# Values of the last block: one expert of each token a row, added up on VectorE

## The chip, the cores and the metric

The kernel runs on one core of one Trainium2 chip. A core has five engines that run side by side, each with its own queue of instructions taken in order: TensorE (PE in the profile), VectorE (DVE), ScalarE (ACT), GpSimd (POOL) and SyncE (SP). SP and POOL mainly issue transfers, which 16 DMA engines carry out. The metric is the device time of one execution in microseconds (us); before the change it was 3333.57 us, the median of 3 runs (3333.47 to 3339.92).

## The reference, cut to what matters

The model is one block: a token mixer (two kinds of attention heads) over 16 meta tokens and 1024 tokens, a residual sum, and then a mixture of 16384 one-neuron experts with a width of 1024, float32 throughout. The change touches the expert part only:

```
# per block of 128 tokens; ids and gate: (128 tokens, 128 chosen experts)
u   = u_emb[ids]                                   # rows of 1024
act = gelu(einsum('ted,td->te', u, xb))            # one key product per token and expert
w   = gate * act
out = einsum('te,ted->td', w, v_emb[ids])          # weighted sum of 128 value rows per token
h_res = h_res + out
```

So each token takes 128 key rows and 128 value rows of 1024 numbers (4 KB), chosen by its own ids.

## The kernel before

The 1024 tokens are worked in four segments of 256 tokens (SEGS), each of two blocks of 128. The middle two segments (DENSE = (1, 2)) compute the experts densely: in a last loop over all 16384 experts, TensorE multiplies with the whole tables. The first and last segment gather: for each block, 128 transfers fetch the key rows and 128 the value rows (gather_rows, L313). The gathers of the last segment run under the dense loop, paced by it.

**The dense loop** (L1254 on) goes over 32 groups of 4 x 128 experts (GRP = 4). For a group, weights (L1215) multiplies the first layer's outputs with the gates (DVE w, L1224), splits each in two parts (ACT Wh, L1227; DVE Wl, L1228); dense_u (L1165) makes the first layer's tiles for a later group (AHEAD = 5 tiles ahead); dense_v (L1232) multiplies with the values in two halves of 512 columns (PE vo, L1246) and adds them up (DVE acc, L1251). A table tile comes through halves (L273): a transfer to raw by SP, a cast on ACT (wh, L279), a difference on DVE (wl, L284); there are four raw buffers (RAW) and two of wh and wl (WH). Of the 32 groups 12 have their first layer computed in earlier stages and stored (spill); for these dense_u only loads w and does a gelu, and TensorE has nothing to do in it. For the others it is 24 products a tile (PE du, L290). The order (L1160) takes 2 stored groups first, then computed ones until as many are left as stored ones, and then one of each in turn.

**The gathers under it.** gather_items (L395) fixes their order: the first block's 128 key rows; then by fours, the first block's values and the second block's keys; then the second block's 128 values. Paced (L1012) takes them: beat (L1198) is called after each first-layer tile (for two) and after each expert tile of dense_v (for one), and asks for 1.08 rows a beat (RATE), each request waiting for the last dense product issued so far; a row is used five steps after it was asked for (LAG). The rows lie in 11 buffers (GATH = 7 and GATHV = 4, room3 L1190).

- A key row tile holds the r-th expert of each token, one token a partition: POOL issues one indirect transfer with 128 row numbers (idx[:, lb, r]), and DVE multiplies it with the block's tokens and sums along the row into column r of actv (L335).
- A value row tile holds the 128 experts of one token, one expert a partition (ask_v, L349, L362). For this the ids are transposed once (idT). When four of them have come (use_v, L368), DVE copies four weight columns into an otherwise zero tile Z (L378), and TensorE multiplies Z with the rows into four groups of 32 columns, two halves each, adding up over 32 steps in G.po (L384); the profile counts 16 products a step. Ahead of the first step, weigh (L338) makes the weights: gelu on ACT, times gate, transposed on TensorE, copied to wT (L347). After the last, the residual comes from h2d into a row buffer, DVE adds G.po to it (L389), and SP stores it.

**What sets the order.** The program gives each instruction its place in the source order, and a planner with a simulated clock puts them in one fixed order for each engine before the kernel runs; dependences become waits. issue_after keeps a row's use behind the last dense product (for TensorE) and the last wl (for DVE) that were issued before it in the source.

Of the kernel before, what the change touches and what calls it, by code (L numbers as in the profile page):

```python
# [9 lines left out]
F32 = mybir.dt.float32  # L10
F32R = mybir.dt.float32r
I32 = mybir.dt.int32
U32 = mybir.dt.uint32
AF = mybir.ActivationFunctionType
OP = mybir.AluOpType
# [4 lines left out]
P = 128  # L20
D = 1024
KT = 8
# [5 lines left out]
NH_M = 4  # L28
# [8 lines left out]
def block_kernel(tc, I, out, dbg=None):  # L37
    nc = tc.nc
    with ExitStack() as ctx:
        _block_kernel(ctx, tc, nc, I, out, dbg)  # L40
# [6 lines left out]
NB = 2  # L47
# [33 lines left out]
GATH = 7  # L81
GATHV = 4

JV = 14

RATE = 1.08
# [5 lines left out]
def _block_kernel(ctx, tc, nc, I, out, dbg):  # L92

    def pool(name, bufs, stack=ctx, **kw):
        return stack.enter_context(tc.tile_pool(name=name, bufs=bufs, **kw))

    cp = pool("const", 1)
    big = pool("big", 1)
    wp = pool("wp", 2)
    pp = pool("peer", 2)  # L100
# [15 lines left out]
    st = pool("state", 1, front)  # L116
# [20 lines left out]
    dve, act, pe, pool_e, sync = nc.vector, nc.scalar, nc.tensor, nc.gpsimd, nc.sync  # L137
# [4 lines left out]
    identr = cp.tile([P, P], F32R, tag="identr", name="identr")  # L142
    dve.tensor_copy(identr, tmpi)
    ident = identr.bitcast(F32)
    negidr = cp.tile([P, P], F32R, tag="negidr", name="negidr")
    dve.tensor_scalar(negidr, tmpi, -1.0, None, op0=OP.mult)
    negid = negidr.bitcast(F32)
    tmpc = cp.tile([P, P], F32, tag="tmpc", name="tmpc")

    mask_st = cp.tile([P, P], F32R, tag="mask_st", name="mask_st")  # L150
    pool_e.memset(tmpc, 0.0)
    pool_e.affine_select(out=tmpc, in_=tmpc, compare_op=OP.is_ge, fill=-BIG, base=0,
                         pattern=[[1, P]], channel_multiplier=-1)
    dve.tensor_copy(mask_st, tmpc)

    tmpc2 = cp.tile([P, P], F32, tag="tmpc", name="tmpc2")
    mask_ts = cp.tile([P, P], F32R, tag="mask_ts", name="mask_ts")
    pool_e.memset(tmpc2, 0.0)
    pool_e.affine_select(out=tmpc2, in_=tmpc2, compare_op=OP.is_ge, fill=-BIG, base=0,
                         pattern=[[-1, P]], channel_multiplier=1)  # L160
    dve.tensor_copy(mask_ts, tmpc2)
    ones = cp.tile([P, P], F32, tag="ones", name="ones")
    pool_e.memset(ones, 1.0)
    blk2 = cp.tile([P, P], F32, tag="blk2", name="blk2")
    pool_e.memset(blk2, 0.0)
    pool_e.memset(blk2[0:64, 0:64], 1.0)
    pool_e.memset(blk2[64:128, 64:128], 1.0)
    eye4 = cp.tile([NH_M, NH_M], F32, tag="eye4", name="eye4")
    dve.tensor_copy(eye4, ident[0:NH_M, 0:NH_M])
    iota_i = cp.tile([P, P], I32, tag="tmpc", name="iota_i")  # L170
    pool_e.iota(iota_i, pattern=[[1, P]], base=0, channel_multiplier=0)
# [12 lines left out]
    for i in range(2):  # L184
        z = cp.tile([P, 4, 63], F32, tag=f"Z{i}", name=f"Z{i}")
# [3 lines left out]

    Zm = []  # L190
    for i in range(2):
        z = cp.tile([P, NB, 66], F32R, tag=f"Zm{i}", name=f"Zm{i}")
        zc = cp.tile([P, 66], F32, tag="tmpc", name="zc")
        pool_e.memset(zc, 0.0)
        pool_e.memset(zc[:, 64:65], -1.0)
        dve.tensor_copy(z, zc.unsqueeze(1).broadcast_to([P, NB, 66]))
        Zm.append(z)
    gmix = cp.tile([P, KT], F32, tag="gmix", name="gmix")
    sync.dma_start(gmix, I["g_mix"])
    gbias = cp.tile([72, 1], F32, tag="gbias", name="gbias")  # L200
    sync.dma_start(gbias, I["g_bias"])
    taps = cp.tile([P, 8, 4], F32, tag="taps", name="taps")
    sync.dma_start(taps, I["taps"])
    gqk = cp.tile([P, 2], F32, tag="gqk", name="gqk")
    sync.dma_start(gqk, I["g_qk"])
    gq8 = cp.tile([P, 1], F32, tag="gq8", name="gq8")
    dve.tensor_scalar(gq8, gqk[:, 0:1], 0.125, None, op0=OP.mult)
    epsc = cp.tile([P, 1], F32, tag="epsc", name="epsc")
    pool_e.memset(epsc, EPS)

    def rsqrt(o, x, scale, t):
# [28 lines left out]
    h2d = dp.tile([SEQ, D], F32, tag="h2d", name="h2d")  # L240
# [20 lines left out]
    for i in range(3):  # L261
        c = slice(i * 512, min(L, i * 512 + 512))
        for e, t in enumerate((oz, zo)):
            t = t[0:NH_F, 0:c.stop - c.start]
# [48 lines left out]
    def gather_rows(S, lb, share, room):  # L313

        b = S.xb0 + lb
        G = SimpleNamespace(S=S, lb=lb, b=b)
        G.actv = pp.tile([P, P], F32, tag="actv", name="actv")
        xn = []

        def ask(r):  # L320
            if r == 0:
                x_ = pp.tile([P, D], F32, tag="xng", name="xng", bufs=1)
                sync.dma_start(x_, xnd[b * P:(b + 1) * P, :])
                xn.append(x_)
            t = room("u", lb, r).tile([P, D], F32, tag="g", name="gu")
            d = pool_e.indirect_dma_start(out=t, out_offset=None, in_=I["peer_u"],  # L326
                                          in_offset=bass.IndirectOffsetOnAxis(ap=S.idx[:, lb, r:r + 1], axis=0))
            return t, d

        def use(r, t):  # L330
            if r % 16 in share:
                pool_e.tensor_tensor(t, t, xn[0], op=OP.mult)
                return lambda: act.activation(t, t, AF.Copy, accum_out=G.actv[:, r:r + 1])
            else:
                dve.scalar_tensor_tensor(t, t, 1.0, xn[0], op0=OP.mult, op1=OP.mult, accum_out=G.actv[:, r:r + 1])  # L335
        G.u = [(lambda r=r: ask(r), lambda t, r=r: use(r, t)) for r in range(P)]

        def weigh():  # L338
            wv = pp.tile([P, P], F32, tag="wv", name="wv", bufs=1)
            gelu = act.activation(wv, G.actv, AF.Gelu)  # L340
            with tc.issue_after(gelu.ins):
                act.preload_act_table_set(EXPLN)
            dve.tensor_mul(wv, wv, S.gate[:, lb, :])
            G.po = po_pool.tile([P, 2, 512], F32, tag="po", name="po")
            pe.transpose(G.po[:, 0, 0:P], wv, ident)
            G.wT = pp.tile([P, 4, 32], F32, tag="wT", name="wT", bufs=1)
            dve.tensor_copy(G.wT, G.po[:, 0, 0:P].rearrange("p (q j) -> p q j", q=4))  # L347

        def ask_v(tok):  # L349
            if S.idT is None:  # L350

                S.idT = []
                tp = po_pool.tile([P, 2, 512], F32, tag="po", name="idt")
                for k in range(NB):
                    idf = pp.tile([P, P], F32, tag="wv", name="idf", bufs=1)
                    dve.tensor_copy(idf, S.idx[:, k, :])
                    pe.transpose(tp[:, k, 0:P], idf, ident)
                    idT = pp.tile([P, P], I32, tag="idT", name="idT")
                    dve.tensor_copy(idT, tp[:, k, 0:P])
                    S.idT.append(idT)  # L360
            t = room("v", lb, tok % 32).tile([P, D], F32, tag="g", name="gv")
            d = pool_e.indirect_dma_start(out=t, out_offset=None, in_=I["peer_v"],  # L362
                                          in_offset=bass.IndirectOffsetOnAxis(ap=S.idT[lb][:, tok:tok + 1], axis=0))
            return t, d

        rows = {}

        def use_v(j, q, t):  # L368


            rows[q] = t
            if q < 3:
                return
            if j == 0:
                weigh()

            z = Zs[j % 2]
            dve.tensor_copy(z[:, :, 31:32], G.wT[:, :, j:j + 1])  # L378
            last = None
            with tc.high_priority():  # L380
                for n in range(2):
                    for q_ in reversed(range(4)):
                        with tc.issue_after(last.ins) if last else nullcontext():
                            last = pe.matmul(G.po[32 * q_:32 * q_ + 32, n, :], z[:, q_, 31 - j:63 - j],  # L384
                                             rows[q_][:, n * 512:(n + 1) * 512], start=(j == 0), stop=(j == 31))
            if j == 31:
                h2 = room("h", lb, j).tile([P, D], F32, tag="g", name="h2o")
                sync.dma_start(h2, h2d[b * P:(b + 1) * P, :])
                dve.tensor_add(h2, h2, G.po.rearrange("p a b -> p (a b)"))  # L389
                sync.dma_start(out[b * P:(b + 1) * P, :], h2)  # L390
        G.v = [(lambda tok=32 * q + j: ask_v(tok), lambda t, j=j, q=q: use_v(j, q, t))
               for j in range(32) for q in range(4)]
        return G

    def gather_items(S, share, room):  # L395

        A, B = (gather_rows(S, lb, share[lb], room) for lb in range(NB))
        yield from A.u
        for i in range(0, P, 4):
            yield from A.v[i:i + 4]  # L400
            yield from B.u[i:i + 4]
        yield from B.v
# [597 lines left out]
    def room0(kind, lb, i):  # L1000

        if kind == "v":
            return gpv if (i >= JV if lb == 0 else i % 2) else gp
        return gp
# [54 lines left out]
    for i in range(-1, len(SEGS)):  # L1059
# [9 lines left out]
        if i >= 0:  # L1069
            S = segs[i]  # L1070
# [114 lines left out]
    gbs.close()  # L1185
    mid.close()
    up = pool("ahead", AHEAD + 1, reuse_waits="tile")
    rows3 = [0]

    def room3(kind, lb, i):  # L1190
# [120 lines left out]
```

## Time and profile before

| what | value |
|---|---|
| median of the runs | 3333.57 us (3333.47 to 3339.92) |
| profiled execution, its own time | 3322.29 us |
| its span, first to last instruction | 3320.4 us |
| mean granted TensorE clock | 0.938 of full speed |
| busy: PE, DVE, ACT, POOL | 3004.0, 2210.0, 1060.2, 1375.3 us |
| moved by DMA | 931.18 MB, mean 280 GB/s |

A busy time is the time in which an engine had an instruction running; instructions that overlap are counted once. In a row of a group of instructions stand the line, the engine and operation, output<-inputs, the shape and the count, then busy us and mean ns of one, then the idle time of the engine just before them, with what ended it. A row of the stretches gives busy time and count for PE, PEld (weight loads), DVE, ACT and POOL, the granted TensorE clock, the DMA engines' share and GB/s. The dense loop runs from about 2024 us to the end; the second block's values are gathered and weighted from about 2985 to 3289 us.

### The profile page before, as it was taken

How to read it: one execution, taken by the hardware profiler on the slowest of the kernel's cores; microseconds unless marked ns; L12 is line 12 of the kernel's file. 1: busy time of each engine (PE TensorE's matmuls, PEld its weight loads, DVE VectorE, ACT ScalarE, POOL GpSimd, SP SyncE). 2: the span in 40 equal slices, each digit the busy share in tenths (PEclk: the TensorE clock that was granted, in tenths of full speed). 3: DMA queues.
4: the chain of work that ended last, by engine and by line, in shares of the span. 5: the costliest groups of instructions: out<-in, count | busy, mean ns of one | idle time of the engine just before them, and what ended most of it. 6: DMA issues, size and time to landing. Idle time of an engine off the chain costs nothing. (4 is left out here: it accounts for less than half of the span.)

```text
span 3320.4 us, 41585 instructions
## 1 busy us (share of the span) xinstructions
PE 3004.0 (90%) x14225; PEld 2196.0 (66%) x14225; DVE 2210.0 (67%) x5506; ACT 1060.2 (32%) x1961; POOL 1375.3 (41%) x1233
## 2 busy tenths in 40 slices
PE   8999789567977889999999876999999999999999
PEld 4566567444754667766468765777777777776666
DVE  3242579996546996556378996888667777674443
ACT  1323423223222322222246683222322322232221
POOL 1000055575456554445564302544435444443442
PEclk9988899878979889999999888999999999999999
DMA  4535488998999988888986637988889999998995
GB/s 136 137 109 138 152 292 276 288 317 292 342 309 360 324 286 246 253 264 312 357 307 232 257 166 263 315 305 318 291 299 366 346 357 340 336 335 317 340 339 199
DMA packets 373816, 931.18 MB, mean 280 GB/s; under 512 B 57268, under 2 KB 143508, under 8 KB 371556
## 3 DMA queue, kind: packets, MB, share of 16 engines
q0 software_dynamic: 161216, 552.56, 47.4%
q1 hardware_dynamic: 212388, 375.96, 33.5%
q8 instruction: 112, 1.84, 0.2%
q14 instruction: 100, 0.82, 0.1%
HBM read 860.91 MB, written 67.47 MB: 280 GB/s over the span
## 5 line engine op out<-in xcount | busy, mean ns | idle before, releaser
L326 POOL DMA_INDIRECT gu<-in_peer_u,idx x512 | 598.5, 1169 | 749.7 <-DVE gu L335 165.9
L362 POOL DMA_INDIRECT gv<-in_peer_v,idT x512 | 547.5, 1069 | 605.0 <-PE po L384 360.7
L335 DVE SCALAR_TENSOR_TENSOR gu<-gu,xng 128x1024 f32<-128x1024 f32 x496 | 614.7, 1255 | 95.9 <-DMA gu<-in_peer_u,idx 89.2
L279 ACT CAST wh<-raw 128x1024 fp32r<-128x1024 f32 x288 | 301.9, 1049 | 822.2 <-PE vo L1246 282.3
L284 DVE TENSOR_TENSOR wl<-raw,wh 128x1024 fp32r<-128x1024 f32 x262 | 323.3, 1234 | 283.3 <-ACT wh L279 235.8
L1246 PE MATMUL vo<-wh,Wh 128*128 128x512 f32 x1024 | 377.6, 397 | 34.7 <-ACT Wh L1227 18.2
L1246 PE MATMUL vo<-wl,Wh 128*128 128x512 f32 x1024 | 403.3, 394 | 0.0
L1246 PE MATMUL vo<-wh,Wl 128*128 128x512 f32 x1024 | 401.4, 393 | 0.0
L303 PE MATMUL fp<-hnh,raw 128*128 128x256 f32 (+1 forms) x1024 | 253.8, 406 | 36.7 <-DVE frs L630 23.1
L384 PE MATMUL po<-gv,Z 128*32 128x512 f32 x2048 | 257.9, 613 | 9.5 <-DMA gv<-in_peer_v,idT 8.4
L1246 PEld LDWEIGHTS vo<-wh,Wh 128*128 128x128 f32 x1024 | 194.6, 190 | 98.6 <-issue 23.5
L303 PEld LDWEIGHTS fp<-hnh,raw 128*128 128x128 f32 x1024 | 203.9, 203 | 78.7 <-DVE frs L630 24.7
L290 PE MATMUL du<-xh,wl 128*128 128x512 f32 x640 | 250.3, 391 | 0.0
L290 PE MATMUL du<-xl,wh 128*128 128x512 f32 x640 | 250.2, 391 | 0.0
L290 PE MATMUL du<-xh,wh 128*128 128x512 f32 x640 | 249.9, 390 | 0.0
L1246 PEld LDWEIGHTS vo<-wl,Wh 128*128 128x128 f32 x1024 | 194.1, 190 | 48.9 <-issue 8.4
L1246 PEld LDWEIGHTS vo<-wh,Wl 128*128 128x128 f32 x1024 | 193.9, 189 | 48.2 <-issue 7.5
L430 PE MATMUL tk<-raw,hnh 128*128 128x512 f32 (+1 forms) x416 | 195.3, 617 | 4.1 <-DMA raw<-in_wt 3.0
L1151 PE MATMUL gout<-A,B 128*128 128x128 f32 x1024 | 155.8, 303 | 43.2 <-DVE A L1149 16.8
L1251 DVE TENSOR_TENSOR acc<-acc,vo 128x512 f32<-128x512 f32 x256 | 167.2, 684 | 32.6 <-PE vo L1246 30.2
L1151 PEld LDWEIGHTS gout<-A,B 128*128 128x128 f32 x1024 | 141.1, 209 | 66.3 <-ACT G L1153 23.4
L1227 ACT CAST Wh<-w 128x512 fp32r<-128x512 f32 x128 | 79.4, 621 | 289.0 <-PE vo L1246 164.4
(407 smaller groups left out, 5165.4 us busy)
## 6 DMA issues: line engine op xcount, KB each, us to landing
raw<-in_ut SPq DMA_DIRECT2D x128, 512.0 KB
raw<-in_peer_v SPq DMA_DIRECT2D x128, 512.0 KB
raw<-in_wf SPq DMA_DIRECT2D x64, 512.0 KB
gd<-G SPq DMA_DIRECT2D x16, 2048.0 KB
Gt<-gd SPq DMA_DIRECT2D x32, 1024.0 KB
raw<-in_wt SPq DMA_DIRECT2D x48, 512.0 KB
raw<-in_wq SPq DMA_DIRECT2D x48, 512.0 KB
raw<-in_wo SPq DMA_DIRECT2D x32, 512.0 KB
```

Of the source, the lines that this page charges most:

```text
L279: seen["act"] = act.copy(h, raw)
L284: seen["dve"] = dve.tensor_sub(l, raw, h.bitcast(F32))
L290: seen["pe"] = pe.matmul(o, w, x[:, c], start=(first and i == 0), stop=(last and i == 2))
L303: pe.matmul(o, raw[:, k * P:(k + 1) * P], xh[:, k, c], start=(k == 0), stop=(k == KT - 1))
L326: d = pool_e.indirect_dma_start(out=t, out_offset=None, in_=I["peer_u"], in_offset=bass.IndirectOffsetOnAxis(ap=S.idx[:, lb, r:r + 1], axi ...
L335: dve.scalar_tensor_tensor(t, t, 1.0, xn[0], op0=OP.mult, op1=OP.mult, accum_out=G.actv[:, r:r + 1])
L362: d = pool_e.indirect_dma_start(out=t, out_offset=None, in_=I["peer_v"], in_offset=bass.IndirectOffsetOnAxis(ap=S.idT[lb][:, tok:tok + 1], ...
L384: last = pe.matmul(G.po[32 * q_:32 * q_ + 32, n, :], z[:, q_, 31 - j:63 - j], rows[q_][:, n * 512:(n + 1) * 512], start=(j == 0), stop=(j ...
L430: pe.matmul(b[0:w, :], xh[:, k, s0:s0 + w], raw[:, k % 2 * 512:(k % 2 + 1) * 512], start=(k == 0), stop=(k == KT - 1))
L1151: pe.matmul(bk[:, u * P:(u + 1) * P], B[:, u, :], A[:, u, :], start=True, stop=True)
L1246: seen["pe"] = pe.matmul(bks[b], w[:, cw], v, start=(ii == 0 and i == 0), stop=(ii == GRP - 1 and i == 2))
L1251: dve.tensor_add(o, o, bks[b])
```

## The change

For the blocks in VDVE, here the second block of the last segment alone, a value row tile holds the r-th expert of each token, as a key row tile does, and its row numbers come from idx as they are. At the first row, the weights are made without a transposition (gelu, times gate), and the block's residual is loaded from h2d into a tile G.sum of its own. Each row is then used by itself: one scalar_tensor_tensor on VectorE adds weight times row to G.sum, in place, with the weight column as a scalar for each partition. After the 128th, G.sum is stored. For that block the index transposition, the transposed weights, Z, the products and the final add go, and so does the change of ScalarE's table behind the gelu. Order, pace, lag and the row buffers stay as they are.

G.sum takes 4 KB in each partition. Constants that only the earlier stages read are placed in a pool that ends with these stages (st in place of cp).

```
+VDVE = ((3, 1),)
...
-    negidr = cp.tile([P, P], F32R, tag="negidr", name="negidr")
+    negidr = st.tile([P, P], F32R, tag="negidr", name="negidr")
...
                 tp = po_pool.tile([P, 2, 512], F32, tag="po", name="idt")
-                for k in range(NB):
+                for k in [k for k in range(NB) if (S.sg, k) not in VDVE]:
                     idf = pp.tile([P, P], F32, tag="wv", name="idf", bufs=1)
...
-        G.v = [(lambda tok=32 * q + j: ask_v(tok), lambda t, j=j, q=q: use_v(j, q, t))
-               for j in range(32) for q in range(4)]
+        def ask_r(r):
+            t = room("v", lb, r).tile([P, D], F32, tag="g", name="gr")
+            d = pool_e.indirect_dma_start(out=t, out_offset=None, in_=I["peer_v"],
+                                          in_offset=bass.IndirectOffsetOnAxis(ap=S.idx[:, lb, r:r + 1], axis=0))
+            return t, d
+
+        def use_r(r, t):
+
+            if r == 0:
+                G.wv = pp.tile([P, P], F32, tag="wr", name="wr", bufs=1)
+                gelu = act.activation(G.wv, G.actv, AF.Gelu)
+                dve.tensor_mul(G.wv, G.wv, S.gate[:, lb, :])
+                G.sum = sums.tile([P, D], F32, tag="gsum", name="gsum", bufs=1)
+                sync.dma_start(G.sum, h2d[b * P:(b + 1) * P, :])
+            dve.scalar_tensor_tensor(G.sum, t, G.wv[:, r:r + 1], G.sum, op0=OP.mult, op1=OP.add)
+            if r == P - 1:
+                sync.dma_start(out[b * P:(b + 1) * P, :], G.sum)
+        if (S.sg, lb) in VDVE:
+            G.v = [(lambda r=r: ask_r(r), lambda t, r=r: use_r(r, t)) for r in range(P)]
+        else:
+            G.v = [(lambda tok=32 * q + j: ask_v(tok), lambda t, j=j, q=q: use_v(j, q, t))
+                   for j in range(32) for q in range(4)]
...
     up = pool("ahead", AHEAD + 1, reuse_waits="tile")
+    sums = pool("sums", 1, reuse_waits="tile")
```

More of the change, by code (lines that the diff above doesn't have):

```diff
@@ L148, in _block_kernel @@
     tmpc = cp.tile([P, P], F32, tag="tmpc", name="tmpc")
-    mask_st = cp.tile([P, P], F32R, tag="mask_st", name="mask_st")
+    mask_st = st.tile([P, P], F32R, tag="mask_st", name="mask_st")
     pool_e.memset(tmpc, 0.0)
@@ L156, in _block_kernel @@
     tmpc2 = cp.tile([P, P], F32, tag="tmpc", name="tmpc2")
-    mask_ts = cp.tile([P, P], F32R, tag="mask_ts", name="mask_ts")
+    mask_ts = st.tile([P, P], F32R, tag="mask_ts", name="mask_ts")
     pool_e.memset(tmpc2, 0.0)
@@ L161, in _block_kernel @@
     dve.tensor_copy(mask_ts, tmpc2)
-    ones = cp.tile([P, P], F32, tag="ones", name="ones")
+    ones = st.tile([P, P], F32, tag="ones", name="ones")
     pool_e.memset(ones, 1.0)
-    blk2 = cp.tile([P, P], F32, tag="blk2", name="blk2")
+    blk2 = st.tile([P, P], F32, tag="blk2", name="blk2")
     pool_e.memset(blk2, 0.0)
@@ L167, in _block_kernel @@
     pool_e.memset(blk2[64:128, 64:128], 1.0)
-    eye4 = cp.tile([NH_M, NH_M], F32, tag="eye4", name="eye4")
+    eye4 = st.tile([NH_M, NH_M], F32, tag="eye4", name="eye4")
     dve.tensor_copy(eye4, ident[0:NH_M, 0:NH_M])
@@ L191, in _block_kernel @@
     for i in range(2):
-        z = cp.tile([P, NB, 66], F32R, tag=f"Zm{i}", name=f"Zm{i}")
+        z = st.tile([P, NB, 66], F32R, tag=f"Zm{i}", name=f"Zm{i}")
         zc = cp.tile([P, 66], F32, tag="tmpc", name="zc")
@@ L197, in _block_kernel @@
         Zm.append(z)
-    gmix = cp.tile([P, KT], F32, tag="gmix", name="gmix")
+    gmix = st.tile([P, KT], F32, tag="gmix", name="gmix")
     sync.dma_start(gmix, I["g_mix"])
-    gbias = cp.tile([72, 1], F32, tag="gbias", name="gbias")
+    gbias = st.tile([72, 1], F32, tag="gbias", name="gbias")
     sync.dma_start(gbias, I["g_bias"])
-    taps = cp.tile([P, 8, 4], F32, tag="taps", name="taps")
+    taps = st.tile([P, 8, 4], F32, tag="taps", name="taps")
     sync.dma_start(taps, I["taps"])
-    gqk = cp.tile([P, 2], F32, tag="gqk", name="gqk")
+    gqk = st.tile([P, 2], F32, tag="gqk", name="gqk")
     sync.dma_start(gqk, I["g_qk"])
-    gq8 = cp.tile([P, 1], F32, tag="gq8", name="gq8")
+    gq8 = st.tile([P, 1], F32, tag="gq8", name="gq8")
     dve.tensor_scalar(gq8, gqk[:, 0:1], 0.125, None, op0=OP.mult)
-    epsc = cp.tile([P, 1], F32, tag="epsc", name="epsc")
+    epsc = st.tile([P, 1], F32, tag="epsc", name="epsc")
     pool_e.memset(epsc, EPS)
```

## The prediction

> **What bounds the kernel now.** First the page: span, busy shares, and the group of the products that the change replaces.
>
> ```profile
> span 3320.4 us, 41585 instructions
> PE 3004.0 (90%) x14225; PEld 2196.0 (66%) x14225; DVE 2210.0 (67%) x5506; ACT 1060.2 (32%) x1961; POOL 1375.3 (41%) x1233
> ...
> L384 PE MATMUL po<-gv,Z 128*32 128x512 f32 x2048 | 257.9, 613 | 9.5 <-DMA gv<-in_peer_v,idT 8.4
> ```
>
> The 2048 products cover four blocks; one block (the change touches one) has 512. TensorE looks like the bound, but shares over the whole span hide the stages, so the second view is busy time by stretch. The first row is the stretch in which the last segment's second block has its values gathered and weighted (from its last key row on VectorE to its last product), the second what follows it, the third an earlier stretch of the same dense loop, where VectorE already takes one gathered row after another (L335) and no L384 product runs; the fourth is the busiest stretch of the DMA engines.
>
> ```profile
> core 0: us, PE busy (x) PEld busy (x) DVE busy (x) ACT busy (x) POOL busy (x), PEclk, DMA share, GB/s
> 2985.00:3289.00 304.00, 304.00 (x1554) 205.83 (x1552) 131.99 (x192) 78.21 (x101) 126.38 (x122) 1.00 0.89 322
> 3289.00:3320.40 31.40, 25.16 (x111) 20.50 (x110) 13.08 (x16) 3.15 (x3) 0.00 (x0) 0.98 0.21 84
> 2052.00:2332.00 280.00, 267.31 (x1155) 219.02 (x1154) 235.77 (x353) 76.56 (x96) 133.36 (x105) 0.98 0.88 308
> ...
> 2500.00:2600.00 100.00, 100.00 (x476) 75.79 (x475) 73.96 (x113) 30.34 (x41) 55.07 (x47) 1.00 1.01 376
> ```
>
> For 304 us TensorE never rests, and VectorE works 132 of them, 43%. The third view is the chain of waits in that stretch. Its pieces are TensorE's own, one after another, with a batch of sixteen L384 products among the dense ones:
>
> ```profile
> 2238.76 21.76 PE du L290 x96
> ...
> 2999.00 1.85 PE po L384 x16
> 3000.86 7.48 PE du L290 x32
> 3008.34 1.85 PE po L384 x16
> 3010.19 7.48 PE vo L1246 x32
> ```
>
> So a batch costs the path 1.85 us (its busy time counts the four column groups' overlap), and a dense product 21.76 / 96 = 0.227 us.
>
> **The change, part by part.** *Removed from TensorE:* 32 batches, 32 x 1.85 = 59.2 us, and one transposition (0.3 us). TensorE's need in the stretch falls from 304 to 304 - 59.5 = 244.5 us.
>
> *Moved on VectorE.* The groups of the stretch:
>
> ```profile
> L284 DVE TENSOR_TENSOR wl<-raw,wh 128x1024 fp32r<-128x1024 f32 x44 | 54.0, 1228 | 79.8 <-ACT wh L279 50.9 <-issue 14.3 <-PE du L290 13.8
> L1251 DVE TENSOR_TENSOR acc<-acc,vo 128x512 f32<-128x512 f32 x56 | 37.2, 685 | 12.6 <-PE vo L1246 11.3 <-issue 1.1
> L1228 DVE TENSOR_TENSOR Wl<-w,Wh 128x512 fp32r<-128x512 f32 x27 | 18.6, 691 | 29.2 <-ACT Wh L1227 19.3 <-PE vo L1246 5.8 <-issue 4.1
> L1224 DVE TENSOR_TENSOR w<-w,Gt 128x512 f32<-128x512 f32 x27 | 18.0, 685 | 2.7 <-ACT w L1173 2.7
> L378 DVE COPY Z<-wT 128x4 f32<-128x4 f32 x32 | 5.5, 175 | 45.4 <-PE po L384 43.3 <-remote 2.1
> L347 DVE COPY wT<-po 128x128 f32<-128x128 f32 x1 | 0.3, 291 | 0.5 <-PE po L345 0.5
> ...
> L1173 ACT ACTIVATE w<-du 128x512 f32<-128x512 f32 x15 | 8.9, 592 | 2.1 <-PE du L290 2.1
> ```
>
> The copies into Z and wT go (5.8 us); the final add (L389) and its load were behind the stretch and cost the path nothing. What comes is 128 weighted adds of 128x1024, each with a scalar read per partition, each reading the sum that the one ahead of it wrote. No such add is in the trace. Four nearest rows price it: the same operation and shape with a per-partition scalar (L849, 1281 ns); row steps that don't depend on each other (L335, each starting 1.14 us after the one ahead, though each lasts 1.22); and a chain that is dependent, in place and with a scalar, but short (L591: 502 ns each, three in 1.58 us).
>
> ```profile
> L849 DVE SCALAR_TENSOR_TENSOR xn<-h2b,ssq,gffn 128x1024 f32<-128x1024 f32 x8 | 10.0, 1281 | 2.9 <-DMA gffn<-in_g_ffn 2.8
> ...
> 2118.66 1.22 DVE L335 SCALAR_TENSOR_TENSOR gu<-gu,xng 128x1024 f32<-128x1024 f32 x1
> ...
> 2119.80 1.22 DVE L335 SCALAR_TENSOR_TENSOR gu<-gu,xng 128x1024 f32<-128x1024 f32 x1
> ...
> L591 DVE SCALAR_TENSOR_TENSOR mqk<-rawc,taps,mqk 128x272 f32<-128x272 f32 x24 | 12.0, 502 | 0.9
> ...
> 63.24 1.58 DVE L591 SCALAR_TENSOR_TENSOR mqk<-rawc,taps,mqk 128x272 f32<-128x272 f32 x3
> ```
>
> Independent steps overlap by 0.08, so the low end is 1.281 - 0.08 = 1.20 us. In the chain a step starts (1.58 - 0.50) / 2 = 0.54 after the one ahead, 0.04 more than it lasts, so the high end is 1.32. Runs of adds and other work will alternate; I take 1.26. VectorE's need: 132.0 - 5.8 + 128 x 1.26 = 287.5 us, with 1.20 it is 279.8, with 1.32 295.2. All three lie above TensorE's 244.5: **the bound of the stretch passes from TensorE to VectorE**, and the most that can come back is 304 - 279.8 = 24 us.
>
> *What VectorE can't use.* The loop alternates groups whose four first-layer tiles are computed (96 products, 21.8 us of TensorE) with groups whose tiles were stored earlier (none). In a computed stretch VectorE has four halves (4 x 1.14 us, at the spacing of L335), four w and four Wl (8 x 0.61, at 0.08 less than they last), and about 4.3 adds (what four beats of dense_v asked five steps earlier, at 1.08 a beat): 4.6 + 4.9 + 5.4 = 14.9 us. TensorE is the bound there, and 6.9 us of VectorE go idle unless it runs ahead into the next stretch, for which it has two tiles (WH = 2). 15 computed tiles are 3.75 such stretches: 0 to 26 us. I take the middle, 13, since the two tiles are worth up to one tile's products (5.4 us) of the 6.9, and nothing says that the order lets them be.
>
> *The added wait.* VectorE now waits for each gathered row, and the halves, Wl and acc steps behind it wait too, and TensorE for them. The earlier stretch shows this price:
>
> ```profile
> L335 DVE SCALAR_TENSOR_TENSOR gu<-gu,xng 128x1024 f32<-128x1024 f32 x105 | 124.8, 1220 | 2.5 <-DMA gu<-in_peer_u,idx 2.5
> ```
>
> 2.5 us for 105 rows is 3 us for 128. The first add also waits for the gelu and for G.sum's load in SP's queue, where the loads ahead of it wait for buffers:
>
> ```profile
> SPq L276 <- DVE wl L284: 213.4, 34, 12.7
> ...
> POOL gv L362 <- PE po L384: 131.5, 28, 11.2
> ```
>
> That is 0 to 12.7 us once; G.sum has a buffer of its own that nothing used before, so the load can go early: 2 us. POOL issues the same 128 gathers of the same size, from idx instead of idT; its 131.5 us of waiting for L384 to free rows become waits for the adds, one row at a time. Its 126 us of work are hidden under 290. Two table loads leave ScalarE (busy 78 of 304), hidden. The second block's index transposition goes (under 1 us), and the constants move in memory with no instruction more or less: nothing, unless the planned order shifts elsewhere, which the trace can't show and which I bound at the runs' own spread.
>
> *Sum:* 287.5 + 13 + 3 + 2 = 305.5 us against 304, that is +1.5. The profiled execution took 3322.29 us, so it gives 3323.8; its time is 11.3 under the median of the runs, 3333.57, and on that the forecast is **3335 us, no change**. A measurement of this kernel tells from no change about 0.2%, 6.7 us: the case's own range is 3327 to 3340.
>
> **The rivals.** *VectorE runs packed (faster).* If it uses the idle stretches, the stage takes 279.8 to 295.2 us; in the middle 287.5, which is 16.5 less: 3317. For it: when TensorE starves, VectorE is busy nearly throughout,
>
> ```profile
> 2170.00:2180.00 10.00, 7.65 (x34) 6.05 (x33) 10.00 (x17) 2.10 (x2) 5.89 (x4) 1.00 1.04 380
> ...
> 2220.00:2230.00 10.00, 7.51 (x27) 5.81 (x26) 9.76 (x17) 1.04 (x1) 2.16 (x2) 0.84 1.00 394
> ```
>
> Against: these are short stretches, and over the 280 us VectorE's share was 84%.
>
> *TensorE's 59 us all come back.* They can't, VectorE's need being above 279 us; if an add cost far less than any row shows, the DMA would stop it: 322 GB/s x 304 us = 97.9 MB, at 376 GB/s 260 us, 44 less: 3290. [...]
>
> *VectorE's queue starves TensorE (slower).* VectorE takes its work in order. An acc step behind a run of adds holds TensorE's banks, a half behind them holds its next weights. It has happened in the earlier stretch, with independent steps:
>
> ```profile
> 2316.29 0.39 PE L1246 MATMUL vo<-wh,Wl 128*128 128x512 f32 x1
> 2319.75 0.77 PE L1246 MATMUL vo<-wh,Wh 128*128 128x512 f32 x1 [3.07 <-DVE acc L1251]
> ...
> 2320.74 0.63 PE L1246 MATMUL vo<-wh,Wl 128*128 128x512 f32 x1
> ...
> 2324.15 0.63 PE L1246 MATMUL vo<-wh,Wh 128*128 128x512 f32 x1
> ...
> 2326.29 0.40 PE L1246 MATMUL vo<-wh,Wl 128*128 128x512 f32 x1
> ```
>
> It decides from the point where VectorE's share falls under 287.5 / 304 = 94.6%, measurably under 92.5%. At 90% the stage takes 319 us, +15: 3349; at the 84% of the earlier stretch 342, +38: 3372. The rows also show that after 3 us without work the products come 0.43 us apart in place of 0.23 for some 14 of them, 2.8 us more a gap; once in each of 3.75 computed stretches that is 10 us on top. [...]
>
> *The change does not do what it says at its start.* If G.sum's load sits behind SP's longest wait, its 12.7 us in place of 2 give +12: 3346.
>
> **How the numbers follow.** No change 0.36; VectorE packed 0.31; all of TensorE's time 0.03; VectorE starving TensorE 0.27; the late load 0.03. Faster 0.34, same 0.36, slower 0.30. The range goes from near the packed case with the cheapest add (-22) to somewhat beyond the starved case at 90% (+20): 3312 to 3354; it leaves out the full gain and the worst shares, about 0.15.
>
> **What would show it.** In the changed kernel: 128 adds at one new line, 1.28 us long and 1.20 to 1.32 from start to start; 1536 products left at L384; in the stretch VectorE 92 to 97% busy and TensorE about 80%, its waits ending in acc and wl steps of VectorE; POOL waiting for the adds. I am wrong if VectorE is under 90% busy there (slower), if the stretch is under 290 us (packed), or if adds take under 1.15 us or wait for DMA by more than 10 us.

## The result and the profile after

The changed kernel took 3296.09 us (median; 3291.49 to 3304.03) against 3333.52 us: a ratio of 0.9893, with a 95% interval of 0.9861 to 0.9925. The ratios in this text are taken over all runs and so differ a little from quotients of medians. Run again beside experiments 6 to 8 it was 0.9914 (0.9889 to 0.9939). It is **faster by some 1%**, where no change was forecast, and the time lies below the range.

The page of the changed kernel, its first lines and the groups that are new or changed:

```profile
span 3293.4 us, 40747 instructions
...
PE 2944.3 (89%) x13711; PEld 2189.0 (66%) x13711; DVE 2353.8 (71%) x5598; ACT 1058.0 (32%) x1959; POOL 1416.5 (43%) x1233
...
L395 POOL DMA_INDIRECT gr<-in_peer_v,idx x128 | 166.6, 1302 | 125.5 <-DVE gsum L407 60.9
L386 PE MATMUL po<-gv,Z 128*32 128x512 f32 x1536 | 192.8, 611 | 9.0 <-DMA gv<-in_peer_v,idT 8.3
```

VectorE has 144 us more, TensorE 60 less, and 512 products are gone. The stretch from 2985 us to the end, and its last 31.4 us, as busy time by engine (the columns are those of the prediction's rows):

```profile
2985.00:3293.40 308.40, 280.54 (x1201) 226.53 (x1199) 295.31 (x313) 81.25 (x104) 164.52 (x126) 0.96 0.91 330
3262.00:3293.40 31.40, 20.70 (x92) 16.81 (x90) 27.17 (x27) 2.13 (x3) 5.12 (x4) 0.89 0.49 174
```

VectorE is busy for 295 of 308 us. Before, the last 31.4 us held 13.1 us of its work; now they hold 27.2, and 15 of the 128 adds:

```profile
L407 DVE SCALAR_TENSOR_TENSOR gsum<-gr,wr,gsum 128x1024 f32<-128x1024 f32 x15 | 19.3, 1284 | 0.3
```

These are its groups from the first add on, and what it waited for in that time:

```profile
L407 DVE SCALAR_TENSOR_TENSOR gsum<-gr,wr,gsum 128x1024 f32<-128x1024 f32 x128 | 164.0, 1281 | 1.3
L286 DVE TENSOR_TENSOR wl<-raw,wh 128x1024 fp32r<-128x1024 f32 x46 | 55.9, 1216 | 2.6 <-ACT wh L281 2.5
L1274 DVE TENSOR_TENSOR acc<-acc,vo 128x512 f32<-128x512 f32 x68 | 43.9, 679 | 1.1 <-PE vo L1269 1.1
L1247 DVE TENSOR_TENSOR w<-w,Gt 128x512 f32<-128x512 f32 x27 | 18.4, 684 | 1.6 <-ACT w L1195 1.6
L1251 DVE TENSOR_TENSOR Wl<-w,Wh 128x512 fp32r<-128x512 f32 x27 | 18.0, 682 | 1.4 <-ACT Wh L1250 1.4
```

The waits behind the arrows come to 6.6 us; before, the idle time ahead of the halves alone had been 79.8 us. The same engine in order of time, from the middle of the stretch and from the end:

```profile
3011.79 1.22 DVE L286 TENSOR_TENSOR wl<-raw,wh 128x1024 fp32r<-128x1024 f32 x1 [0.48 <-ACT wh L281]
3012.93 1.28 DVE L407 SCALAR_TENSOR_TENSOR gsum<-gr,wr,gsum 128x1024 f32<-128x1024 f32 x1
3014.12 0.68 DVE L1247 TENSOR_TENSOR w<-w,Gt 128x512 f32<-128x512 f32 x1
3014.72 1.28 DVE L407 SCALAR_TENSOR_TENSOR gsum<-gr,wr,gsum 128x1024 f32<-128x1024 f32 x1
...
3275.30 5.23 DVE L407 SCALAR_TENSOR_TENSOR gsum<-gr,wr,gsum 128x1024 f32<-128x1024 f32 x4
3280.70 1.37 DVE L1274 TENSOR_TENSOR acc<-acc,vo 128x512 f32<-128x512 f32 x2 [0.16 <-PE vo L1269]
3281.98 1.28 DVE L407 SCALAR_TENSOR_TENSOR gsum<-gr,wr,gsum 128x1024 f32<-128x1024 f32 x1
3283.18 1.28 DVE L1274 TENSOR_TENSOR acc<-acc,vo 128x512 f32<-128x512 f32 x2
3284.38 5.24 DVE L407 SCALAR_TENSOR_TENSOR gsum<-gr,wr,gsum 128x1024 f32<-128x1024 f32 x4
```

Mostly a step of another kind stands between two adds, and that step then starts 1.19 to 1.20 us after the add has started, in 70 of 91 cases. Four in a row take 5.24 us, the last of them 1.28: (5.24 - 1.28) / 3 = 1.32 from start to start. The adds run beside the last group's products and on past them: VectorE's last two acc steps begin at 3283.2, and four adds follow them.

Profiles differ by up to 16 us in when they reach the second block's part, so for what the change touches there is a steadier measure: **from the last key row on VectorE to the end of the span**. It was 3320.4 - 2985.2 = 335.2 us before; after, with the last key row at 2995.4, it is 298.0, and 298.0 again in the second profile. That is 37.2 us less.

```profile
L335 DVE SCALAR_TENSOR_TENSOR gu<-gu,xng x496: 1195/1218/4096, 422.9 to 2985.2; 128x1024 f32<-128x1024 f32 x166
L337 DVE SCALAR_TENSOR_TENSOR gu<-gu,xng x496: 1194/1218/4121, 417.9 to 2995.4; 128x1024 f32<-128x1024 f32 x166
```

The rows are those of the key rows' instructions before and after: shortest, median and longest in ns, and the first and last start. Below, "the part" is the time by this measure. In both kernels the same 2285 products with the values lie between the loop's start and this point. The planned orders of the changed kernel and of the one that has all of it but the adds are alike on every engine up to this part, but for the second block's index transposition and the place of G.sum's load.

### The profile page after: what moved, and what is told of

Same layout as the page of the kernel before. It is cut to its first block, busy times and chain, and to the rows that moved or that the text cites. A ratio compares the mean times of both kernels' runs of the same rounds, so it can differ in the third digit from the quotient of the medians.

```text
span 3293.4 us, 40747 instructions
## 1 busy us (share of the span) xinstructions
PE 2944.3 (89%) x13711; PEld 2189.0 (66%) x13711; DVE 2353.8 (71%) x5598; ACT 1058.0 (32%) x1959; POOL 1416.5 (43%) x1233
## 4 chain that ended last, share of the span: by engine, by line
PE 57%; DVE 17%; DMA 11%; issue 7%; ACT 4%; POOL 3%; SPq 0%; POOLq 0%; DVEq 0%; ACTq 0%
PE vo L1269 16%; PE du L292 8%; PE fp L292 6%; DVE gu L337 6%; PE tk L452 6%; DMA gu<-in_peer_u,idx 5%; PE po L386 5%; PE fp L305 5%; POOL gu L328 2%; PE q L292 2%; PE pv L806 2%; PE gout L1173 2%; PE q L305 1%; PE fs L793 1%; DMA gv<-in_peer_v,idT 1%
## 5 line engine op out<-in xcount | busy, mean ns | idle before, releaser
L364 POOL DMA_INDIRECT gv<-in_peer_v,idT x384 | 414.0, 1078 | 435.8 <-PE po L386 215.7
L1269 PEld LDWEIGHTS vo<-wl,Wh 128*128 128x128 f32 x1024 | 197.8, 193 | 54.9 <-DVE wl L286 10.7
L395 POOL DMA_INDIRECT gr<-in_peer_v,idx x128 | 166.6, 1302 | 125.5 <-DVE gsum L407 60.9
L386 PE MATMUL po<-gv,Z 128*32 128x512 f32 x1536 | 192.8, 611 | 9.0 <-DMA gv<-in_peer_v,idT 8.3
```

The lines of the kernel that those rows point to most:

```text
L1269: seen["pe"] = pe.matmul(bks[b], w[:, cw], v, start=(ii == 0 and i == 0), stop=(ii == GRP - 1 and i == 2))
```

## The experiments

Theory A: TensorE's 59 us go, and the time is then what VectorE needs from the last key row to the very end, tail included. Rival B: the DMA engines are the bound after the change. Rival C: the gain comes from the memory layout or the order elsewhere.

**1. All but the core.**

```
-VDVE = ((3, 1),)
+VDVE = ()
```

> All of the change except its core: the constants lie in the pool that ends early and the code for rows by expert rank is there, but no block uses it; every block is weighted by TensorE products. Theory A (the whole gain is the 59 us of products gone from TensorE, limited by what VectorE can carry up to the very end of the kernel): within 0.3% of the kernel before. Rival C (the gain, or a third of it or more, comes from the memory layout or from the order planned for earlier stages): 12 to 37 us below the kernel before.

Measured: ratio 1.0018 (0.9994 to 1.0042) to the kernel before. The measure from the last key row (2980.2) to the end (3315.8) is 335.6 us, against 335.2. Rival C is out.

**2. Adds of 4 columns.**

```
-            dve.scalar_tensor_tensor(G.sum, t, G.wv[:, r:r + 1], G.sum, op0=OP.mult, op1=OP.add)
+            dve.scalar_tensor_tensor(G.sum[:, 0:4], t[:, 0:4], G.wv[:, r:r + 1], G.sum[:, 0:4], op0=OP.mult, op1=OP.add)
```

> The changed kernel, but each weighted add takes only the first 4 of 1024 columns (so 1020 columns of the second block get no expert output): gathers, waits and row buffers stay, the adds cost VectorE about 0.2 us in place of 1.28. Theory A: VectorE is no longer the bound, TensorE is (244.5 us in the stretch and 23 behind it, against 308 from 2985 us to the end now): 25 to 40 us below the changed kernel, about 3262. Rival B (the DMA rate is the bound after the change, 330 GB/s mean and 380 to 404 in places): at most 7 us below the changed kernel.

Measured: 0.9887 (0.9847 to 0.9927). This misses what A expected and is the size that rival B had given: with next to nothing left of the adds, the ratio is within the interval of the changed kernel's, and the part is 292.2 us, 6 below 298.0. Either the DMA engines were the bound all along, or the bound passed on to them and hardly anything lay between; run 4 tells the two apart. In the chain of waits of this run a table load stands for 26 us, where the changed kernel's chain has only transfers of rows (under 5% of it in this part) and that of the kernel before none:

```profile
3013.44 26.18 DMA raw<-in_peer_v
3039.63 1.05 ACT wh L281
3040.73 17.15 PE vo L1269 x68
```

The DMA engines are busy throughout, in the stretch around it (first row) and from the last key row until the last value rows land at about 3254 us (second row); what follows is mainly the products of the last loads. The two columns at the end are share and GB/s:

```profile
2985.00:3100.00 115.00, 109.14 (x473) 89.64 (x472) 63.92 (x123) 34.24 (x45) 63.30 (x58) 0.99 1.03 383
2988.30:3255.00 266.70, 250.27 (x1066) 203.17 (x1065) 148.09 (x286) 76.06 (x100) 133.16 (x122) 0.97 0.98 364
```

**3. Adds of 512 columns.** The same edit with 0:512.

> The changed kernel, but each weighted add takes only the first 512 columns (the other 512 of the second block get no expert output): 0.6 to 0.68 us an add, VectorE's need from 2985 us on falls from 302 to about 220 us, well under TensorE's 268. Theory A: like the run with 4 columns, 25 to 40 us below the changed kernel, and within 8 us of that run. Rival B: at most 7 us below the changed kernel. If VectorE's share matters even where it is not the bound, it lies between: some 15 us above the 4-column run.

Measured: 0.9884 (0.9845 to 0.9924), the part 290.0 us. Like the run with 4 columns, as A had it, but 8 us under the changed kernel and not 25. From half the width down VectorE's share makes no difference that shows.

**4. Rows of half the length.** Only 512 columns of each value row are gathered, and the add reads them twice.

```
-            d = pool_e.indirect_dma_start(out=t, out_offset=None, in_=I["peer_v"],
+            d = pool_e.indirect_dma_start(out=t[:, 0:512], out_offset=None, in_=I["peer_v"].rearrange("e (a c) -> (e a) c", a=2),
...
-            dve.scalar_tensor_tensor(G.sum, t, G.wv[:, r:r + 1], G.sum, op0=OP.mult, op1=OP.add)
+            bc = [P, 2, 512]
+            s2 = G.sum.rearrange("p (a c) -> p a c", a=2)
+            dve.scalar_tensor_tensor(s2, t[:, 0:512].unsqueeze(1).broadcast_to(bc), G.wv[:, r:r + 1], s2, op0=OP.mult, op1=OP.add)
```

> The changed kernel, but each gathered value row of the second block has 512 columns (half the bytes: 33 MB less), and the add reads them twice to make its 1024, so its cost stays; the values are not those of the reference. Theory A (VectorE is the bound): within 8 us of the changed kernel. Rival B (DMA): 33 MB at 376 GB/s is 88 us of transfer less in a 308 us stretch, so it falls to TensorE's bound, 25 to 40 us below the changed kernel.

Measured: 0.9908 (0.9879 to 0.9936), the part 299.4 us against 298.0. Taking 33 MB off the DMA engines brings nothing while the adds are whole: rival B is out for the changed kernel. The last dense product starts at 3258.5 us in this run and the last add at 3290.9, so at the end VectorE alone is left.

**5. The changed kernel again**, as the base of the next three.

> The changed kernel once more, on the chip of the runs beside it, as their base. Any theory: 0.986 to 0.993 of the kernel before.

Measured: 3290.28 us, 0.9914 (0.9889 to 0.9939).

**6. No adds beside the last group.** The kernel is the changed one but for the place of the last group's steps on VectorE.

```
-            dve.scalar_tensor_tensor(G.sum, t, G.wv[:, r:r + 1], G.sum, op0=OP.mult, op1=OP.add)
+            S.last = dve.scalar_tensor_tensor(G.sum, t, G.wv[:, r:r + 1], G.sum, op0=OP.mult, op1=OP.add)
...
-        W = weights(g)
+        with tc.issue_after(segs[-1].last.ins) if g == NG - 1 else nullcontext():
+            W = weights(g)
```

> The changed kernel with one more rule for the order: VectorE's work for the last group of experts (its w, Wl and acc steps) comes behind the 128th add, so that no add can lie beside that group's 22 us of products, as the prediction took for granted of the stretch that ends at 3289 us. Theory A (the adds slide into the last 30 us, where VectorE had been busy 13 us of 31): 15 to 25 us above the changed kernel. Rival (the place of the adds at the end is worth nothing): within 4 us.

Measured: 3306.02 us, 15.7 above the changed kernel beside it; 0.9977 (0.9962 to 0.9992) to the kernel before. The part takes 315.2 us in place of 298.0. VectorE's end in this run:

```profile
3257.24 14.49 DVE L407 SCALAR_TENSOR_TENSOR gsum<-gr,wr,gsum 128x1024 f32<-128x1024 f32 x11
3271.65 2.49 DVE L1247 TENSOR_TENSOR w<-w,Gt 128x512 f32<-128x512 f32 x4
3274.05 2.50 DVE L1251 TENSOR_TENSOR Wl<-w,Wh 128x512 fp32r<-128x512 f32 x4
3282.29 1.22 DVE L286 TENSOR_TENSOR wl<-raw,wh 128x1024 fp32r<-128x1024 f32 x1 [5.74 <-ACT wh L281]
```

Adds first, then the last group's weights, and TensorE waits for them, 20.9 us at one go:

```profile
PE vo L1269 <- ACT Wh L1250: 20.9, 1, 20.9
```

With the tail closed to the adds, a gain of about 0.2% is left. But for the last group's weights, 5 us of VectorE's work that come behind the adds too, this is the order that the forecast had described. Its part is still 22 us under the forecast's 305.5 + 31.4 = 336.9, so the tail alone doesn't account for the miss.

**7. Both cuts: adds of 4 columns, rows of half the length.**

> Both cuts at once: gathered value rows of 512 columns for the second block and adds of 4 columns (the second block gets almost no expert output). If the run with 4-column adds stopped short of the 59 us of products because the DMA engines became its bound, this one is 8 to 16 us below it, 45 to 59 us below the kernel before. If it stopped because TensorE had nothing more to give, it is within 4 us of it.

Measured: 3264.35 us, 0.9852 (0.9824 to 0.9881), 51.5 us below the kernel before, the part 267.9 us, 24 below the run with 4-column adds alone (by the ratios 12). So that one did stop at the DMA engines. TensorE hardly rests here, and the transfers are down to 246 GB/s:

```profile
2985.00:3263.70 278.70, 271.38 (x1203) 222.69 (x1201) 167.32 (x313) 81.29 (x104) 136.00 (x126) 1.00 0.72 246
```

**8. 1.2 rows a beat.**

```
-RATE = 1.08
+RATE = 1.2
```

> The changed kernel with 1.2 rows asked a beat in place of 1.08: the first block's values and the second block's keys come earlier, when TensorE is the bound and VectorE 71% busy, so more of the adds find an idle VectorE. Theory A: 5 to 20 us below the changed kernel, unless the DMA engines (350 GB/s there already) can't take it, then no change or up to 10 us above.

Measured: 3271.19 us, 19 below the changed kernel beside it, 0.9866 (0.9845 to 0.9887) to the kernel before: the fastest of the kernels that compute everything. The first add now starts at 2947.2 us, the last at 3264.4:

```profile
L407 DVE SCALAR_TENSOR_TENSOR gsum<-gr,wr,gsum x128: 1272/1281/1322, 2947.2 to 3264.4; 128x1024 f32<-128x1024 f32 x128
```

From first to last start they take 317 us where they had 290, with TensorE busy for 351 of the 355 us from 2900 on:

```profile
2500.00:2900.00 400.00, 393.76 (x1867) 295.91 (x1866) 282.50 (x422) 116.81 (x154) 187.21 (x164) 0.99 0.95 345
2900.00:3255.00 355.00, 350.95 (x1550) 285.67 (x1549) 332.15 (x370) 106.60 (x137) 196.16 (x141) 1.00 0.94 335
```

The loop itself, from its first product with the values to the end of the span, is 1257.2 us long here and 1268.7 in run 5, so the profiles show 11.5 of the 19 us there. The rest lies ahead of the loop, where no row is paced, and isn't shown to come from the pace.

**9 and 10. 1.35 and 1.5 rows a beat.**

> The changed kernel with 1.35 rows a beat in place of 1.08 (1.2 gave 19 us under the changed kernel). Theory A: the adds of the second block start earlier still and spread over more of the loop; as long as the DMA engines keep up, 5 to 15 us below the run with 1.2; if they are the bound of the first two thirds (they were at 0.95 to 0.97 there with 1.2), within 5 us of it or above.

> The changed kernel with 1.5 rows a beat. Theory A: no better than 1.35, since rows are then asked faster than 11 buffers and the DMA engines can turn them over; 0 to 25 us above the run with 1.35.

Measured: 0.9891 (0.9859 to 0.9922) and 0.9907 (0.9874 to 0.994). By these ratios both lie 0.25 to 0.4% above the run with 1.2, the first against what A hoped for, but their intervals overlap with that run's. With 1.35 the last add starts at 3233.0 us and the tail is empty again. Yet the loop is no longer for it: 1258.9 us with 1.35 and 1254.4 with 1.5, against 1257.2 with 1.2. In its first 480 us TensorE is busy for 453 us with 1.35 (first row) and for 457 with 1.2 (second row):

```profile
2032.10:2512.10 480.00, 453.12 (x1992) 355.77 (x1993) 369.95 (x560) 128.03 (x161) 260.46 (x202) 0.96 0.91 327
2012.20:2492.20 480.00, 456.71 (x2006) 362.01 (x2007) 366.80 (x547) 130.37 (x164) 228.61 (x184) 0.97 0.89 310
```

What differs is when the loop starts: at 2032.1 us with 1.35 and 2042.5 with 1.5, at 2012.2 with 1.2, though TensorE's order ahead of it is the same in all three. So a pace beyond 1.2 brings nothing more in the loop; that it costs something isn't shown.

**11. The kernel before with 1.2 rows a beat.**

> The kernel before (TensorE weights both blocks) with 1.2 rows a beat. Theory A: TensorE is the bound of the loop from about 2350 us on whatever the order of the gathers, so within 0.3% of the kernel before (10 us either way). Rival: the quicker pace is worth its 19 us by itself, without the adds on VectorE.

Measured: 1.0033 (1.0014 to 1.0052). The quicker pace alone is worth nothing, it costs a little; it helps only where VectorE carries the rows.

**12. Both blocks on VectorE.**

```
-VDVE = ((3, 1),)
+VDVE = ((3, 0), (3, 1))
```

> The changed kernel with both blocks of the last segment weighted on VectorE: 128 adds more (128 x 1.24 = 159 us) and the other 59 us of products gone. Theory A: from 2332 us on VectorE's need rises from about 745 to about 900 us of 960; it just fits if packed as tightly as in the second block's stretch, so it ends within 12 us of the changed kernel either way, and TensorE's second 59 us are worth nothing. If TensorE were still what limits the first block's stretch, 20 to 50 us below the changed kernel.

Measured: 0.9876 (0.9842 to 0.991), that is within the interval of the changed kernel's ratio. The second 59 us of TensorE come to nothing that could be told, as expected. From the first block's values on both engines are nearly full (VectorE 93%, TensorE 92%), but at the end VectorE alone is left, with 19 adds in a row behind the last product:

```profile
2332.00:3285.00 953.00, 878.44 (x3764) 712.96 (x3763) 886.62 (x1077) 269.50 (x348) 497.13 (x385) 0.97 0.94 337
3256.40 25.05 DVE L407 SCALAR_TENSOR_TENSOR gsum<-gr,wr,gsum 128x1024 f32<-128x1024 f32 x19
```

## Why the prediction was wrong

**The step that failed is the limit of the sum**: the forecast took the stretch to end at 3289 us with its 31.4 us behind it untouched, and said that the most that can come back is 304 - 279.8 = 24 us. The adds were not bound to the stretch of the products that they replaced. The planner placed them as rows came, they slid beside the last group's products, and the 18 us that VectorE had free there took them in. Run 6 closes the tail and loses 15.7 us, leaving a gain of 0.2%.

**The second step that failed is the idle time.** Of the 13 us for stretches where TensorE is the bound, 3 for rows and 2 for the load, the trace shows 6.6 us of waits in all, and none for a row. The rival "VectorE runs packed" had this right. The row that spoke against it, VectorE's 84% in the earlier stretch, was no evidence: there TensorE was busy for 267 of the 280 us, and VectorE's idle time was what that left over.

With both put right, and the add at its cheap end, the forecast's own terms come to the result: need 279.8, plus the tail's 13.1, less the final add of 1.2 that goes, plus 6.6 of waits, is 298.3 us; measured 298.0. Of the 39 us between 336.9 and this, the tail makes 19.5, the idle time 11.4 and the price of the add 7.7. That the sum meets to 0.3 us is luck. VectorE's busy time in the part is 286.3 us and not 291.7, since neighbouring steps overlap (a half lasts 1.22 us and the next step starts 1.14 after it), and the sum has no term for 1.3 us of idle time ahead of adds, nor for the 3.8 us from the end of the last add to the end of the span, in which G.sum is stored.

Point by point:

- *512 products go, 59 us of TensorE.* Right that they go: 1536 are left. The 59 us were too low, which cost the forecast nothing, since TensorE isn't the bound after the change. In the part TensorE was busy for 329.0 us before and for 260.6 in run 7, at a granted clock of 1.00 both times, so a batch of sixteen cost 68 / 32 = 2.1 us and not 1.85. In the prediction's chain 32 dense products behind a batch take 7.48 us, where 32 x 0.227 is 7.26. Run 7 as a whole, with little in their place, is 51.5 us faster.
- *The add costs 1.20 to 1.32, taken 1.26.* The bounds were right: 1.19 to 1.20 ahead of another step, 1.32 in a chain, 1281 ns each as in the row for L849. Mostly it is the low end: of 127 adds with a step behind them 36 have another add there.
- *The bound passes to VectorE.* Right for the changed kernel (run 4: less to transfer brings nothing; 295 of 308 us busy). The DMA engines are next, 6 to 8 us behind (runs 2, 3 and 7). The forecast had them as the limit if an add cost next to nothing, 260 us at 376 GB/s in place of 304, 44 less. That was right: in run 2 they take 267 us at 364 GB/s, and the part is 43.0 us shorter than before.
- *Rows land in time, POOL is covered.* Right: VectorE was idle ahead of the adds for 1.3 us in all, though the chain has two rows that land just as their adds start, and POOL waited 60.9 us for adds, hidden.
- *The load of G.sum.* It was issued at 1920.5 us, a thousand us early. The rival in which it is late was out from the start.
- *VectorE starves TensorE.* It does: TensorE waits 17.2 us of the 308 for halves and their casts (8.9, 5.4 and 2.9), with the granted clock at 0.96; another 10.7 us lie behind its last product. Two neighbouring stretches of the changed kernel, with gaps and without:

```profile
3120.00:3150.00 30.00, 25.54 (x100) 20.32 (x101) 28.35 (x30) 5.75 (x6) 17.27 (x14) 0.89 0.97 332
3150.00:3180.00 30.00, 30.00 (x134) 24.83 (x133) 29.93 (x31) 8.48 (x11) 17.26 (x14) 1.00 0.90 336
```

  With 4.5 us of gaps the clock is at 0.89, without at 1.00. The longest of these gaps is 3.0 us, from 3121.2 on, with one of 1.6 just ahead of it; the granted clock is 0.50 from 3122.5 to 3129.3, which is 5.1 us of slow products. In the kernel before, the gap of 3.07 us in the prediction's rows went with a clock of 0.50 from 2319.0 to 2325.8, and 6 us of slow products. So the loss was of the same kind in both, 6.8 us at half clock each time; how long a gap it takes was not shown. VectorE is 28 to 30 us busy in both stretches and waits only 6.6 us in all, so the slow products can have cost little while it is the bound.
- *Layout and planned order: nothing.* Right (run 1).

What stays open: the profiles reach the second block's part at 2980 to 2997 us. Of those at 1.08 rows a beat (run 12 left aside), the two without the adds are the earliest (2980.2 and 2985.2), though the orders ahead of it are alike. Counted from the start of the loop they need 968 and 961 us to this point, the others 965 to 976. No run tells whether that is chance. If it isn't, the 37.2 us of the part are more than the whole gain: from the loop's start to the end of the span the profiles have 1296.1 and 1304.0 us without the adds, 1272.7 and 1268.7 with them.

## What to carry to other kernels

When work moves to an engine that becomes the bound, sum its need to the end of the kernel and not to the end of the stretch that the old work filled: the new work may slide into whatever free time comes later. Idle time of an engine measured where another is the bound need not tell how tightly it packs once it is the bound itself: here it was 16% there and 4% after the change. And after such a move set the pace again: 1.2 rows a beat cost the old kernel 0.3%; the new one ran 19 us faster with it, 11.5 of them in the loop.

## What the runs showed of the hardware

- A chain of dependent, in-place VectorE adds of 128x1024 in float32 started a step every 1.32 us in the changed kernel (mean of 36 pairs, 1.30 to 1.36); a step of another kind behind such an add started 1.19 to 1.20 us after it had started in 70 of 91 pairs, 1.24 to 2.23 in the others. Behind a half, 1.22 us long, the next step started 1.13 to 1.14 us after it (47 pairs). So an add with another step behind it mostly took 1.20 us of VectorE's time there, in place of 1.32.
- The DMA engines held 383 GB/s over 115 us with gathers of 4 KB rows and 512 KB loads mixed (run 2), and one load of 512 KB then stands in the chain of waits for 26 us.
- Three times in the changed kernel's last 300 us, ahead of its last product, TensorE's granted clock was halved for 6.8 us, each time within a gap of 2.6 to 3.0 us that had one of 1.6 to 2.1 us just ahead of it.
- Three bounds (VectorE, DMA, TensorE) lay within about 30 us of each other in a part of 298: taking one away was worth 6 us, one that wasn't the bound 0, two at once 30.
